# Loading Q and K as float32 four heads at a time, with the cast on GpSimd and all stores on one queue

## The chip, the cores and the metric

The kernel runs on one core of a Trainium2 chip. The metric is the time of one execution on the device in microseconds (us). The profile gives a span (first to last instruction), which is about 1.9 us shorter than the time of the same execution.

## The reference

```python
q, k: float32, shape (8, 12, 1024, 64)          # 96 heads in all
out = np.einsum('bhid,bhjd->bhij', q, k)         # float32, shape (8, 12, 1024, 1024)
```

The inputs are 50.33 MB together and the output is 402.65 MB, 4 MB (4,096 KB) for each head. Writing the output is nearly all of the work.

## The kernel before

For each head, Q and K are loaded by two DMAs of GpSimd's queue that cast float32 to float16 on the way, transposed on TensorE, and multiplied. VectorE and ScalarE (ACT) move the 512-wide results from PSUM (the memory that TensorE writes its results to) into a 4 MB output tile, and one DMA stores it.

```python
in_pool  = ... bufs=24      # float16 Q and K of one head each: 12 heads ahead
out_pool = ... bufs=5       # output tiles of 4 MB
for bh in range(96):
    q_sb = in_pool.tile([P, NT, D], F16); k_sb = ...        # P=128, NT=8, D=64
    nc.gpsimd.dma_start(out=q_sb, in_=qf[bh].rearrange("(p t) d -> p t d", p=P))
    nc.gpsimd.dma_start(out=k_sb, in_=kf[bh].rearrange("(p t) d -> p t d", p=P))
    # ... 4 transposes of Q, 16 of K (each K block twice, for both halves of the array),
    # ... copied to qT_sb and kT_sb by VectorE (cut) ...
    o_sb = out_pool.tile([P, NT, S], F32)
    for n in range(2):
        for t in range(NT):
            # ... matmul to ps [P, 512]; copy to o_sb by VectorE (7) or ACT (9) (cut) ...
    out_eng = nc.sync if bh % 2 == 0 else nc.scalar
    out_eng.dma_start(out=of[bh].rearrange("(p t) j -> p (t j)", p=P), in_=o_sb)
```

A partition of a load is 8 rows of 64 numbers: 2 KB read, 1 KB written. A partition of a store is one contiguous run of 32 KB. So each store is 128 packets of 32 KB, 8 for each of 16 DMA engines (the trace has 12,288 such packets for 96 heads).

## Time and profile before

| | before |
|---|---|
| median of its first 3 runs | 1075.96 us (1073.93 to 1078.4) |
| span of the profiled execution | 1077.5 us |
| busy: TensorE, VectorE, ACT, GpSimd | 61%, 52%, 44%, 9% |
| HBM traffic over the span | 420 GB/s |
| mean store packet (32 KB), fastest class of them | 1224.7 ns, 1213 ns |
| load packets (1 KB written) | 24,576 of about 99 ns |

These are lines of the profile's page of the kernel before. The DMA line has the mean busy share of the 16 DMA engines in tenths, in 40 equal slices of the span, and the GB/s line what they moved, in bytes as they are written (a casting load counts half of what it reads: 25.18 MB in q0's line, of 50.33 MB read). A queue's line has packets, MB, and the time of its packets as a share of 16 engines' span. The last lines are DMA issues: KB each, and the median us from issue to landing.

```profile
span 1077.5 us, 9569 instructions
...
DMA  9999999999999999999999999999999999999998
GB/s 230 391 426 420 428 415 386 422 355 421 422 385 392 422 425 360 421 423 397 367 422 426 347 421 423 386 396 364 421 417 391 393 422 421 353 419 423 353 425 373
...
q1 hardware_dynamic: 6912, 201.33, 43.8%
q10 hardware_dynamic: 6912, 201.33, 43.6%
q0 software_dynamic: 27648, 25.18, 14.5%
q8 instruction: 27, 0.44, 0.1%
...
HBM read 50.33 MB, written 402.65 MB: 420 GB/s over the span
...
out_dram<-o_sb SPq DMA_DIRECT2D x48, 4096.0 KB, 25.6
...
q_sb<-in_q_dram POOLq DMA_DIRECT2D x96, 128.0 KB, 39.5
```

The DMA line says what bounds the kernel: 9 everywhere, 8 in the last slice. Q1 and q10 are the stores of SP and ACT, q0 the loads. The shares add up to more than 100% because several small load packets can be in flight on one engine. A load of 128 KB takes 39.5 us to land: it shares the engines with stores.

From the view of waits of the same kernel (engine, line, what it waited for: us in total, times, longest us):

```profile
ACT o_sb L82 <- PE ps L71: 564.9, 363, 24.3
...
PEld L56 <- DMA k_sb<-in_k_dram: 210.4, 31, 16.9
```

The engines wait for loads, and behind them for each other. As the DMA engines have work nearly all the time, these waits are a result of the bound, not the bound.

The view of windows, with the stretch in us, then each engine's busy time, the granted clock, the DMA share (1.00 is 16 engines) and GB/s:

```profile
core 0: us, PE busy (x) PEld busy (x) DVE busy (x) ACT busy (x) POOL busy (x), PEclk, DMA share, GB/s
...
10.00:20.00 10.00, 8.89 (x43) 2.81 (x41) 7.38 (x13) 6.15 (x12) 7.79 (x15) 1.00 1.28 224
...
1050.00:1060.00 10.00, 0.00 (x0) 0.00 (x0) 0.00 (x0) 0.00 (x0) 0.00 (x0) 0.50 0.99 426
1060.00:1068.00 8.00, 0.00 (x0) 0.00 (x0) 0.00 (x0) 0.00 (x0) 0.00 (x0) 0.50 1.05 451
1068.00:1076.00 8.00, 0.00 (x0) 0.00 (x0) 0.00 (x0) 0.00 (x0) 0.00 (x0) 0.50 0.77 332
```

After compute has ended, the engines drain their last stores at full rate almost to the end. In the packet records, all 16 are busy until 1.6 us before the last store packet ends.

### The profile page before, as it was taken

What the parts mean: (1) busy time and instruction counts of PE and PEld (TensorE: products, weight loads), DVE (VectorE), ACT (ScalarE), POOL (GpSimd) and SP (SyncE); (2) the same over time, 40 slices, a digit from 0 to 9 for tenths busy, and PEclk for the clock granted to TensorE, in tenths of its full rate; (3) what the DMA queues carried; (4) which work ended last, traced back from release to release, by engine and by line L of the source; (5) the groups of instructions that cost most, each with busy time, mean ns of one, the idle gap of its engine ahead of it and who ended that gap; (6) DMA issues with size and microseconds to landing.
All of it is one profiled execution on the core that took longest, in us unless ns stands there. A gap on an engine that the chain in (4) does not pass through costs nothing.

```text
span 1077.5 us, 9569 instructions
## 1 busy us (share of the span) xinstructions
PE 654.1 (61%) x3456; PEld 211.4 (20%) x3456; DVE 564.9 (52%) x864; ACT 469.5 (44%) x865; POOL 102.1 (9%) x198
## 2 busy tenths in 40 slices
PE   6888428458718627817693784665871862684470
PEld 2222102112202202202221221111220220221120
DVE  5686426447618625816473482544761862483360
ACT  4475315336506514615362462434650651463360
POOL 6100001020002002000200200102000100200000
PEclk9995555656556755855555565555655675565555
DMA  9999999999999999999999999999999999999998
GB/s 230 391 426 420 428 415 386 422 355 421 422 385 392 422 425 360 421 423 397 367 422 426 347 421 423 386 396 364 421 417 391 393 422 421 353 419 423 353 425 373
DMA packets 41519, 428.44 MB, mean 398 GB/s; under 512 B 4608, under 2 KB 29184, under 8 KB 29184
## 3 DMA queue, kind: packets, MB, share of 16 engines
q1 hardware_dynamic: 6912, 201.33, 43.8%
q10 hardware_dynamic: 6912, 201.33, 43.6%
q0 software_dynamic: 27648, 25.18, 14.5%
q8 instruction: 27, 0.44, 0.1%
q14 instruction: 20, 0.16, 0.0%
HBM read 50.33 MB, written 402.65 MB: 420 GB/s over the span
## 4 chain that ended last, share of the span: by engine, by line
PE 34%; another core or an unknown queue 25%; DMA 21%; DVE 15%; issue 2%; ACT 1%; POOL 0%; DVEq 0%; POOLq 0%; ACTq 0%
PE ps L71 21%; DMA q_sb<-in_q_dram 13%; DVE o_sb L78 7%; DVE kT_sb L62 6%; PE t_ps L56 5%; DMA k_sb<-in_k_dram 5%; PE t_ps L57 4%; PE t_ps L54 4%; DMA out_dram<-o_sb 3%; DVE qT_sb L61 1%; ACT o_sb L82 1%; POOL q_sb L47 0%; POOL k_sb L48 0%; DVEq L78 0%
## 5 line engine op out<-in xcount | busy, mean ns | idle before, releaser
L82 ACT COPY o_sb<-ps 128x512 f32<-128x512 f32 x864 | 468.2, 595 | 577.4 <-PE ps L71 564.9
L78 DVE COPY o_sb<-ps 128x512 f32<-128x512 f32 x672 | 427.3, 682 | 212.3 <-ACT o_sb L82 124.4
L71 PE MATMUL ps<-kT_sb,qT_sb 64*128 64x512 f16 x1536 | 485.7, 552 | 39.0 <-DVE o_sb L78 29.6
L56 PE MATMUL t_ps<-ident,k_sb 128*64 128x128 f16 x768 | 143.1, 303 | 192.7 <-DMA k_sb<-in_k_dram 192.7
L61 DVE COPY qT_sb<-t_ps 128x512 f16<-128x512 f16 x96 | 40.2, 418 | 269.4 <-PE ps L71 258.6
L54 PE MATMUL t_ps<-ident,q_sb 128*128 128x128 f16 x384 | 68.5, 280 | 160.5 <-DMA q_sb<-in_q_dram 114.2
L57 PE MATMUL t_ps<-ident,k_sb 128*64 128x128 f16 x768 | 151.5, 303 | 0.0
L71 PEld LDWEIGHTS <-qT_sb 64*128 64x128 f16 x1536 | 94.5, 105 | 195.1 <-issue 162.2
L56 PEld LDWEIGHTS <-k_sb 128*64 128x64 f16 x768 | 74.0, 144 | 250.6 <-DMA k_sb<-in_k_dram 210.4
L62 DVE COPY kT_sb<-t_ps 128x1024 f16<-128x1024 f16 x96 | 116.4, 1213 | 0.0
L57 PEld LDWEIGHTS <-k_sb 128*64 128x64 f16 x768 | 76.9, 143 | 107.7 <-issue 107.7
L47 POOL DMA_DIRECT2D q_sb<-in_q_dram x96 | 51.1, 532 | 423.9 <-PE ps L71 146.8
L48 POOL DMA_DIRECT2D k_sb<-in_k_dram x96 | 50.9, 530 | 423.7 <-PE t_ps L57 205.3
L54 PEld LDWEIGHTS <-q_sb 128*128 128x128 f16 x384 | 31.6, 113 | 280.7 <-issue 145.9
L82 ACT ACT_TABLE_LOAD x1 | 1.3, 1283 | 0.7 <-PEq L103 0.7
masks.py:199 POOL TENSOR_SCALAR_AFFINE_SELECT ident<-ident 128x128 f16<-128x128 f16 x1 | 0.3, 305 | 0.1
masks.py:197 POOL MEMSET ident<- 128x128 f16 x1 | 0.2, 204 | 0.3 <-POOLq L103 0.3
L103 POOL MEMSET const-float32-0.0<- 128x1 f32 x1 | 0.1, 98 | 0.2 <-issue 0.2
L103 POOL MEMSET const-bfloat16-1.0<- 128x1 bf16 x1 | 0.1, 101 | 0.0
L103 POOL MEMSET const-uint8-127<- 128x1 uint8 x1 | 0.1, 101 | 0.0
L103 POOL MEMSET const-float32-1.0<- 128x1 f32 x1 | 0.1, 98 | 0.0
## 6 DMA issues: line engine op xcount, KB each, us to landing
out_dram<-o_sb SPq DMA_DIRECT2D x48, 4096.0 KB, 25.6
out_dram<-o_sb ACTq DMA_DIRECT2D x48, 4096.0 KB, 26.8
q_sb<-in_q_dram POOLq DMA_DIRECT2D x96, 128.0 KB, 39.5
k_sb<-in_k_dram POOLq DMA_DIRECT2D x96, 128.0 KB, 34.7
```

What stands on the lines that cost most here:

```text
L47: nc.gpsimd.dma_start(out=q_sb, in_=qf[bh].rearrange("(p t) d -> p t d", p=P))
L48: nc.gpsimd.dma_start(out=k_sb, in_=kf[bh].rearrange("(p t) d -> p t d", p=P))
L54: nc.tensor.transpose(qT_ps[:, e], q_sb[:, 2 * e : 2 * e + 2], ident)
L56: nc.tensor.transpose(kT_ps[0:64, t], k_sb[:, t], ident)
L57: nc.tensor.transpose(kT_ps[64:128, t], k_sb[:, t], ident)
L61: nc.vector.tensor_copy(out=qT_sb, in_=qT_ps)
L62: nc.vector.tensor_copy(out=kT_sb, in_=kT_ps.transpose([0, 2, 1]))
L71: nc.tensor.matmul(ps, qT_sb[h : h + 64, e], kT_j[h : h + 64, n * 512 : (n + 1) * 512],)
L78: nc.vector.tensor_copy(out=o_sb[:, t, n * 512 : (n + 1) * 512], in_=ps)
L82: nc.scalar.copy(out=o_sb[:, t, n * 512 : (n + 1) * 512], in_=ps)
L103: nc = _bacc.Bacc("TRN2", target_bir_lowering=False, num_devices=1)
```

## The change

The intent: fewer and larger load packets (8 KB instead of 1 KB written), loads issued well ahead, wider evictions (1024 instead of 512), and one queue for all stores. A partition holds 32 consecutive rows of a batch of four heads; the rows are put in order by interleaved transposes. The loads move to ACT's queue and stay float32, without a cast on the way, and GpSimd casts each head's slab. The core of the diff, cut:

```diff
-    in_pool = ... bufs=24 ; out_pool = ... bufs=5 ; po_pool = ... bufs=6 ([P, 512])
+    in_pool = ... bufs=3 (four heads) ; half_pool = ... bufs=3 ; out_pool = ... bufs=4 ; po_pool = ... bufs=3 ([P, 1024])
+    sizes = [1, 1, 2] + [4] * 23
-        nc.gpsimd.dma_start(out=q_sb, in_=qf[bh].rearrange("(p t) d -> p t d", p=P))   # float16 tile
-        nc.gpsimd.dma_start(out=k_sb, in_=kf[bh].rearrange("(p t) d -> p t d", p=P))
+            self.q_sb = in_pool.tile([P, GMAX * NT, D], F32, tag="q")
+            self.k_sb = in_pool.tile([P, GMAX * NT, D], F32, tag="k")
+            for src, dst in ((qf, self.q_sb), (kf, self.k_sb)):
+                nc.scalar.dma_start(out=dst[:, : self.R], in_=src[rows].rearrange("(p r) d -> p r d", p=P))
+            nc.gpsimd.tensor_copy(out=q_h, in_=self.q_sb[:, slab])
+            nc.gpsimd.tensor_copy(out=k_h, in_=self.k_sb[:, slab])
+            # transposes of q_h, k_h as before; then copies that interleave:
+            for g in range(G):
+                nc.vector.tensor_copy(out=qT[:, g, :, :, a], in_=t_ps[:, 0:4, ms])
+            nc.vector.tensor_copy(out=kT[:, :, :, a], in_=t_ps[:, 4:12].rearrange("c t (g m) -> c g m t", g=G))
-                ps = po_pool.tile([P, 512], F32)       # 7 copies by VectorE, 9 by ACT
+                ps = po_pool.tile([P, S], F32)         # 3 copies of 1024 by VectorE, 5 by ACT
-        out_eng = nc.sync if bh % 2 == 0 else nc.scalar
-        out_eng.dma_start(out=of[bh]..., in_=o_sb)
+            nc.sync.dma_start(out=of[bh]..., in_=o_sb)
... (batches; loads issued three batches ahead; each batch's transposes run among the scores of the one before) ...
```

## The prediction

> **What bounds it now.** The DMA engines. In the page's 40 slices DMA is at 90% or more in all but the last; PE is busy 61%, DVE 52%, ACT 44%. The trace's packet records show 16 packets in flight practically always; idle DMA time sums to about 7 us: 2.6 us before the first load, 3.2 us near 1013 us (the last loads land late, the stores run dry), 1.4 us at the end. The compute waits (ACT on PE 565 us, weight loads on k_sb 210 us, view of waits) follow from full queues: 1 KB load packets take turns with 32 KB store packets, so loads trickle until stores run low.
>
> **Costs from the trace.** A store packet is 32 KB in 1213 ns undisturbed: 432 GB/s for 16 engines; the Trainium skill (DMA: Bandwidth & Descriptors, "Where 436 GB/s comes from") gives 435 as the ceiling, and the trace agrees. 402.65 MB of stores need 932 us. Loads: 24,576 packets that read 2 KB and write 1 KB, 96 ns each (150 us of 16 engines), but they overlap, up to 20 in flight: effectively 75 to 80 ns. Stores slow a little beside them (mean 1225 ns). The span leaves some 130 us for loads and semaphores, against 116 us for 50.33 MB at 432 GB/s: small packets cost only about 14 us. The halved write traffic of the casting load saved nothing; bytes read set the pace.
>
> **The change.** Load packets become 8 KB (less in the first three batches), a quarter as many; 8 KB packets of the instruction queue took 309 ns, so 6,144 are an estimated 113 to 119 us. The dry stretch near 1013 us should go: an 8 KB load packet per 32 KB store packet gets a fifth of the engines, issued two batches ahead. Against it, a slower start. The first store left after 19.7 us, with prefetching loads filling the time; now about eight heads (4.2 MB, 10 us) are loaded before it, and the first head needs load, cast, transposes, copies and eviction in sequence, about 14 us: 2 to 4 us more idle DMA. A single SP store queue should cost nothing: where one queue was alone the engines stayed full, also across its DMA boundaries.
>
> **Off the path.** Per head (11 us budget): ACT 5 copies of 1024, estimated 1.02 us each from 595 ns for 512: 5.1 us. DVE 3 at 1.2, kT copy 1.2, four 128-column qT copies at 0.28: 6.0 us. PE as before, 6.8 us. GpSimd two 512-element casts; the skill (GPSIMD Engine Reference, 3.1) has 512 elements in 0.77 us at best: 1.6 to 2.2 us. All fit, and four output buffers give 37 us of slack.
>
> **Sum.** Stores 932 to 938, loads 113 to 119, semaphores and instruction fetch 2 to 3, start 5 to 6, end 3: 1055 to 1069. I predict 1060 us (ratio 0.985), 1050 to 1072 in 8 of 10. Chances: over 2% faster 0.16, within 2% 0.78, over 2% slower 0.06.
>
> **What would show it.** DMA at 9 in nearly all slices; HBM about 427 GB/s over the span (420 now); load queue share about 11% (14.5% now); some 6,500 load packets; first store near 14 us; no wait of PE for loads; mean store packet near 1220 ns.
>
> **What would make it wrong.** Faster: large load packets overlap store packets more than small ones. Slower: the chain of cast, transposes, single transpose buffer and DVE copies exceeding 11 us per head at the throttled clock (granted mean 0.60), or bubbles between stores of one queue: then DMA slices below 9 and store waits on DVE or ACT.

## More of the kernel before

The experiments ran on three chips, four kernels to a chip; the kernel before was rerun each time, with medians of 1077.2, 1077.85 and 1077.38 us, so kernels of different groups are compared by their ratios to it.

## The result, and the profile after

| | before | after |
|---|---|---|
| median of 4 runs | 1076.89 us (1073.93 to 1078.4) | 1081.55 us (1080.08 to 1081.68) |
| ratio, 95% interval | 1 | 1.0042 (1.0024 to 1.0060) |
| span of the profiled execution | 1077.5 us | 1079.7 us |

A ratio here and below is the mean time of one kernel's runs over that of the other's of the same rounds, so it is not quite the ratio of the medians. The change is within 2%, as predicted likeliest, but it is slightly slower where 1.5% faster was predicted, and 1081.55 lies outside the range of 1050 to 1072.

The page after:

```profile
span 1079.7 us, 9227 instructions
...
DMA  8999999999999999999999999999999999999993
GB/s 294 428 431 431 425 426 433 426 434 424 430 439 421 431 434 422 434 429 427 434 432 429 433 425 436 427 428 431 429 432 428 426 431 438 429 428 436 429 432 171
...
q1 hardware_dynamic: 13824, 402.66, 86.9%
q10 hardware_dynamic: 7488, 50.33, 11.3%
q8 instruction: 27, 0.44, 0.1%
...
HBM read 50.33 MB, written 402.65 MB: 420 GB/s over the span
...
L79 POOL CAST q_h<-q_sb 128x512 f16<-128x512 f32 x96 | 59.2, 616 | 776.0 <-PE t_ps L83 744.1
...
out_dram<-o_sb SPq DMA_DIRECT2D x96, 4096.0 KB, 36.1
```

In between, the GB/s line is what was hoped for: 421 to 439, without the dips to 347 of before (there the engines ran casting load packets, of which the line counts half the bytes that are read, so a part of the dips is a matter of counting). But the first slice is 8, and the last is 3, with 171 GB/s instead of 373. One slice is 27 us. The waits:

```profile
ACT o_sb L119 <- DMA out_dram<-o_sb: 264.2, 54, 6.9
...
POOL q_h L79 <- DMA q_sb<-in_q_dram: 4.3, 4, 2.3
```

Compute now waits for free output tiles (ACT, 264 us in all), and almost never for loads: GpSimd's casts, their only reader, waited 4.3 us for Q in the whole run, and 2.5 us for K. So stores are always queued ahead, in up to four tiles. The windows:

```profile
10.00:20.00 10.00, 6.91 (x53) 2.89 (x54) 6.27 (x8) 4.49 (x5) 3.84 (x7) 0.97 0.67 256
...
1050.00:1060.00 10.00, 0.00 (x0) 0.00 (x0) 0.00 (x0) 0.00 (x0) 0.00 (x0) 0.50 0.99 426
1060.00:1068.00 8.00, 0.00 (x0) 0.00 (x0) 0.00 (x0) 0.00 (x0) 0.00 (x0) 0.50 0.37 160
1068.00:1076.00 8.00, 0.00 (x0) 0.00 (x0) 0.00 (x0) 0.00 (x0) 0.00 (x0) 0.50 0.07 29
```

From 1068 to 1076 us the DMA share is 0.07, and one engine of 16 is 0.0625: **one DMA engine works alone** on the last stores, at 29 GB/s, and the other 15 have finished. The packet records say the same. In the table, "tail" is the time from the moment at which the first of the 16 engines has no store packet left to the end of the last packet. (On one engine, a packet begins 3 to 4 ns before the end of the one before it. That overlap is taken off, as otherwise 15 engines can count as 16.) The times are on the records' own clock, on which the span begins at about 10.4 us (before) and 10.7 us (after).

| | first store packet | 16 engines busy until | last store packet ends | tail |
|---|---|---|---|---|
| before | 30.1 us | 1085.0 us | 1086.6 us | 1.6 us |
| after | 33.7 us | 1070.1 us | 1088.9 us | 18.7 us |

So the change did work: the engines were kept together for 15 us less (1070.1 against 1085.0), though the first store came 3.6 us later. Then the tail took it all back. (The profiled execution of the kernel before is not among its timed runs, and with 1077.5 us of span it is some 2.5 us slower than their median; so up to 2.5 of the 15 us may be chance.)

The records carry no engine number. But on one engine a packet begins where the one before ended, and a packet of 4 bytes, for the semaphore, follows the 8 packets of each store. So the packets can be chained into 16 sequences. At 866 us, when the loads had ended, one sequence still had 181 store packets to do and the other fifteen had 169 to 174. And the lag grew over the run: the sixteen parts of one store landed within 3.6 us of each other at 45 us, and from 3.1 us early to 10.9 us late, against the median, at 617 us. In the kernel before, the spread was 2.6 us in the median store and never over 5.9 us, and it did not grow.

The chains of the kernel after also say where the lag comes from. From 60 us on, each has 750 or 751 store packets. The late engine's take 1240.8 ns in the mean (up to 1035 us), the others' 1217.6 to 1222.6 ns. Packets of 1230 to 1333 ns cost the late engine about 17 us in all, and the others 0.5 to 2 us each. Instruction fetches are not the reason: this chain has none of 16 KB, and two of 8 KB, one of them after its last store.

### The profile page after: what moved, and what is told of

Same layout as the page of the kernel before. It is cut to its first block, busy times and chain, and to the rows that moved or that the text cites. A ratio compares the mean times of both kernels' runs of the same rounds, so it can differ in the third digit from the quotient of the medians.

```text
span 1079.7 us, 9227 instructions
## 1 busy us (share of the span) xinstructions
PE 672.6 (62%) x3456; PEld 213.2 (20%) x3456; DVE 566.9 (52%) x758; ACT 469.0 (43%) x481; POOL 118.8 (11%) x198
## 3 DMA queue, kind: packets, MB, share of 16 engines
q10 hardware_dynamic: 7488, 50.33, 11.3%
## 4 chain that ended last, share of the span: by engine, by line
DMA 79%; PE 8%; ACT 7%; DVE 2%; issue 1%; ACTq 0%; POOL 0%; SPq 0%
DMA out_dram<-o_sb 75%; PE ps L111 7%; ACT o_sb L119 7%; DMA k_sb<-in_k_dram 3%; PE t_ps L86 1%; DVE kT L97 1%; DVE o_sb L117 1%; DVE qT L96 1%; PE t_ps L83 1%; DMA q_sb<-in_q_dram 0%; PE t_ps L87 0%; ACTq L119 0%; POOL q_h L79 0%; SPq L120 0%
## 5 line engine op out<-in xcount | busy, mean ns | idle before, releaser
L119 ACT COPY o_sb<-ps 128x1024 f32<-128x1024 f32 x480 | 467.7, 1014 | 571.1 <-DMA out_dram<-o_sb 264.2
L111 PE MATMUL ps<-kT,qT 64*128 64x512 f16 x1536 | 524.1, 604 | 235.2 <-ACT o_sb L119 168.0
L117 DVE COPY o_sb<-ps 128x1024 f32<-128x1024 f32 x288 | 352.0, 1223 | 379.8 <-PE ps L111 221.3
L111 PEld LDWEIGHTS <-qT 64*128 64x128 f16 x1536 | 98.5, 109 | 613.6 <-issue 593.8
L96 DVE COPY qT<-t_ps 128x128 f16<-128x128 f16 (+1 forms) x374 | 122.1, 470 | 98.7 <-PE t_ps L87 98.7
L79 POOL CAST q_h<-q_sb 128x512 f16<-128x512 f32 x96 | 59.2, 616 | 776.0 <-PE t_ps L83 744.1
L97 DVE COPY kT<-t_ps 128x1024 f16<-128x1024 f16 x96 | 118.8, 1237 | 0.0
L87 PE MATMUL t_ps<-ident,k_h 128*64 128x128 f16 x768 | 103.9, 312 | 0.0
L86 PE MATMUL t_ps<-ident,k_h 128*64 128x128 f16 x768 | 103.4, 314 | 0.0
L86 PEld LDWEIGHTS <-k_h 128*64 128x64 f16 x768 | 78.7, 167 | 22.0 <-issue 20.8
L87 PEld LDWEIGHTS <-k_h 128*64 128x64 f16 x768 | 78.5, 165 | 5.9 <-issue 5.9
L80 POOL CAST k_h<-k_sb 128x512 f16<-128x512 f32 x96 | 59.1, 616 | 51.5 <-PE t_ps L87 48.6
## 6 DMA issues: line engine op xcount, KB each, us to landing
q_sb<-in_q_dram ACTq DMA_DIRECT2D x23, 1024.0 KB, 17.2
k_sb<-in_k_dram ACTq DMA_DIRECT2D x23, 1024.0 KB, 28.6
```

Source lines behind the costliest of these rows:

```text
L79: nc.gpsimd.tensor_copy(out=q_h, in_=self.q_sb[:, slab])
L80: nc.gpsimd.tensor_copy(out=k_h, in_=self.k_sb[:, slab])
L86: nc.tensor.transpose(t_ps[0:64, 4 + t], rows, ident)
L87: nc.tensor.transpose(t_ps[64:128, 4 + t], rows, ident)
L96: nc.vector.tensor_copy(out=qT[:, g, :, :, a], in_=t_ps[:, 0:4, ms])
L97: nc.vector.tensor_copy(out=kT[:, :, :, a], in_=t_ps[:, 4:12].rearrange("c t (g m) -> c g m t", g=G),)
```

## The experiments

The theories, as they stood before the runs:
- A: one DMA engine is slower than the rest, and the change lets it fall behind. Before, stores ran dry so often that all engines waited for each other; now four tiles are queued and nothing waits.
- B: one SP store queue is the cause.
- C, and F later: the float32 loads themselves are the cause.
- D: the depth of the output buffers lets the lag grow, so fewer would help.
- G: the casts on GpSimd disturb the DMA engines. I: instruction fetches do. R: fetches that fall on one engine do. Q: it is which queue issues the loads.

Every kernel below gave correct results. The edits are against the kernel after.

### e1: stores alternate between SP and ACT again (theory B)

```diff
-            nc.sync.dma_start(
+            (nc.sync if bh % 2 == 0 else nc.scalar).dma_start(
```

> Edit: the changed kernel, but stores alternate between SP and ACT as before. In the trace of the changed kernel 15 of 16 DMA engines finish their last store between 1059 and 1067 us of the span and one runs alone to 1078. Theory A (one engine needs some 2% longer for each store packet while the others run ahead, and nothing in the changed kernel makes them wait for it): no change, 1078 to 1084 us, the tail of about 12 us stays. Theory B (the single SP queue lets the engines drift apart or leaves bubbles): the tail goes, 1064 to 1072 us.

Measured: 1131.7 us, ratio 1.0520 (1.0492 to 1.0547). The DMA and GB/s lines of its page:

```profile
DMA  8989999999999999999989998997998999799998
GB/s 308 399 354 404 431 427 439 423 419 426 426 408 384 424 406 385 407 377 424 400 353 411 426 427 338 426 426 321 410 431 359 410 419 428 319 424 429 427 428 377
```

Both numbers were missed. The tail is gone, as B had it (2.4 us), but B's gain did not come, so B falls. Slices of 7 and 8 appear in the middle: the stores run dry, about every four heads, and at these points a lag is made good (in between, the parts of one store land up to 24 us apart). Two reasons are likely, and no run separates them: two stores now share the engines, so both finish late, and with four tiles there is too little left to fill the gap; and loads sit behind stores in ACT's queue (a 1 MB load of K takes 36.6 us to land here, 28.6 us in the kernel after). The Trainium skill (DMA: Bandwidth & Descriptors, "Rules for kernel authors") says that spreading DMAs over several issuing engines does not help bandwidth; this run agrees, and it cost 5% here, where the loads are on ACT's queue too.

### e2: the loads cast again, four heads at a time, by GpSimd's queue; no casts on GpSimd (theories C, F)

```diff
-            self.q_sb = in_pool.tile([P, GMAX * NT, D], F32, tag="q")     # and k_sb
+            self.q_sb = in_pool.tile([P, GMAX * NT, D], F16, tag="q")     # and k_sb
-                nc.scalar.dma_start(
+                nc.gpsimd.dma_start(
-            nc.gpsimd.tensor_copy(out=q_h, in_=self.q_sb[:, slab])        # and k_h
+            q_h = self.q_sb[:, slab]                                      # and k_h
```

> Edit: the changed kernel with its four-head batches, but loaded by casting GpSimd DMAs straight into float16 tiles, no float32 tiles and no casts on GpSimd. Theory A: load packets still read 8 KB, so the load share stays near 11% and the slow engine still ends last: 1076 to 1084 us with a tail over 8 us. Theory C (the float32 writes of the loads, twice the bytes into SBUF, are what slows store packets): mean store packet falls from 1220 to about 1214 ns, 1065 to 1073 us.

Measured: 1071.04 us, ratio 0.9949 (0.9928 to 0.9971), faster than both kernels. The tail is 10.7 us and the first store packet comes 4.5 us earlier than in the kernel after. A alone had 1076 to 1084 and missed: what the loads do has a part in how far the engine falls behind. C's range holds the time, but not for C's reason: the mean store packet did not fall to 1214 ns, it is 1223.0 ns. This edit changes three things at once (queue, bytes written, GpSimd's work); e5, e6 and e9 take them apart.

### e3: two output buffers instead of four (theory D)

```diff
-    out_pool = ctx.enter_context(tc.tile_pool(name="out_pool", bufs=4))
+    out_pool = ctx.enter_context(tc.tile_pool(name="out_pool", bufs=2))
```

> Edit: the changed kernel with 2 output buffers in place of 4, so no engine can run more than about one store ahead of the slowest. Theory A: the slow engine sets the pace either way; the tail shrinks to under 5 us, the fast engines idle along the way instead, and the time stays within 1% of 1081 (1076 to 1092), more only if the compute of one head (about 8 us) no longer hides behind one store (9.7 us). If the tail were a separate loss (theory D, a one-off delay of one engine that adds to the end), removing it would give 1066 to 1071 us.

Measured: 1109.0 us, ratio 1.0299 (1.0271 to 1.0327). The tail is gone (1.8 us). But the time is paid elsewhere, and more of it: the parts of one store land within 1.7 us of each other in the median, so the engines run in step, and stores run dry. Its GB/s line:

```profile
GB/s 303 428 433 425 386 439 395 407 416 405 435 416 420 418 401 418 402 418 417 401 429 411 415 434 403 419 417 388 437 393 419 416 383 418 417 401 434 420 422 378
```

D, that fewer buffers would be a gain, falls. For A this is a sign, though its number was missed: with few buffers no lag can accumulate, and there is no tail. It is not a measure of the lag, as two tiles also leave compute less room behind the stores, and how the 27 us are shared between the two is not shown.

### e4: one store without the partitions that were taken for the slow engine's (theory A)

```diff
-            nc.sync.dma_start(out=dst, in_=src)
+            parts = [(0, 120), (120, 128)] if bh == 88 else [(0, 128)]
+            for lo, hi in parts:
+                nc.sync.dma_start(out=dst[lo:hi], in_=src[lo:hi])
```

> Edit: the changed kernel, with the store of one head (88) cut into partitions 0 to 119 and 120 to 127. By the Trainium skill (DMA: Bandwidth & Descriptors, section on the semaphore increment) these use the 15 and the 8 lowest engines, so the sixteenth engine is spared 8 packets (9.7 us), the lowest eight get one more each (1.2 us). The skill also says that engines 7 and 15 are usually slower. If the slow engine is number 15: tail falls from 12 us to about 2, time 1070 to 1073 us. If it is another (7 or any other): 1081 to 1084 us. Either way theory A says that the end is set by one engine's queue alone.

Measured: 1100.3 us, ratio 1.0221 (1.0199 to 1.0244), unclear against the 2% line. The time decides nothing. The divided store's packets ran slowly, with about 140 us of engine time lost around it, and two engines ended late instead of one (the tail is 21.9 us). The chains of its trace tell more. After 866 us one chain has 160 store packets, eight fewer than any other (168 to 182): the spared engine. It is not the slow one, whose packets of 1230 to 1333 ns mark it; that one has 182 and ends last. So the slow engine is not the sixteenth, if the parts went to the engines as the page has it.

### e5: the casts on VectorE instead of GpSimd (theory G)

```diff
-            nc.gpsimd.tensor_copy(out=q_h, in_=self.q_sb[:, slab])        # and k_h
+            nc.vector.tensor_copy(out=q_h, in_=self.q_sb[:, slab])        # and k_h
```

> Edit: the changed kernel with its float32 loads, but the two casts of a head run on VectorE instead of GpSimd. The packet records of the changed kernel, strung together by the end of one packet and the start of the next, show that one engine loses some 20 us over the run to store packets of 1230 to 1320 ns while compute is active (others lose about 5), and none once compute has ended. Theory G (GpSimd's work slows that engine): 1068 to 1074 us, tail under 8 us. Theory F (the float32 writes of the loads do): 1078 to 1083. Theory I (the slowing grows with the number of instructions executed, whatever they are): 1079 to 1082. VectorE stays off the path (6.0 us a head, plus two casts at an estimated 0.4 to 0.6 us).

Measured: 1086.07 us, ratio 1.0075 (1.0060 to 1.0091). The tail is 17.7 us, nearly that of the kernel after. G falls. The loss of some 4 us is at the start: the first store packet comes 5.4 us later (39.1 us), as the casts take their turn among VectorE's other work.

### e6: casting loads as in e2, but GpSimd copies float16 to float16 where it cast (theories F, G)

```diff
-            self.q_sb = in_pool.tile([P, GMAX * NT, D], F32, tag="q")     # and k_sb
+            self.q_sb = in_pool.tile([P, GMAX * NT, D], F16, tag="q")     # and k_sb
-                nc.scalar.dma_start(
+                nc.gpsimd.dma_start(
```

> Edit: the changed kernel, but with casting GpSimd DMAs into float16 tiles, and the two GpSimd copies of a head kept (float16 to float16). Against the run without these copies (1071 us) this adds GpSimd work and two instructions a head, but no float32 bytes. Theory G: 1077 to 1082 us, with a tail over 10 us. Theory F: 1070 to 1073. Theory I: 1070 to 1073 (2 of about 96 instructions a head).

Measured: 1071.83 us, ratio 0.9942 (0.9925 to 0.9959), as e2. GpSimd's work costs nothing; the gain of e2 is in the loads. From its windows (same columns as above):

```profile
1050.00:1060.00 10.00, 0.00 (x0) 0.00 (x0) 0.00 (x0) 0.00 (x0) 0.00 (x0) 0.50 0.94 406
1060.00:1068.00 8.00, 0.00 (x0) 0.00 (x0) 0.00 (x0) 0.00 (x0) 0.00 (x0) 0.50 0.15 66
```

There is still a tail, of 9.9 us, about half of that of the kernel after.

### e7: 48 tiny GpSimd instructions more for each head (theory I)

```diff
+            for x in range(24):
+                nc.gpsimd.memset(q_h[:, 0, x : x + 1], 1.0)     # overwritten by the cast after it
+                nc.gpsimd.memset(k_h[:, 0, x : x + 1], 1.0)
             nc.gpsimd.tensor_copy(out=q_h, in_=self.q_sb[:, slab])        # and k_h
```

> Edit: the changed kernel with 48 one-column memsets on GpSimd per head ahead of the casts, into the tiles that the casts then overwrite: about 50% more instructions in the program, few bytes. Theory I: the lag of the slow engine grows by half, 1088 to 1095 us, tail 18 us or more. Theory G: 1080 to 1084. Theory F: 1080 to 1082.

Measured: 1093.03 us, ratio 1.0138 (1.0123 to 1.0153). The number is the one that theory I expected, but the trace shows another way to it, so I is not confirmed. Theory I had it that the many slightly long store packets (16 to 120 ns over 1213 ns) come from fetches; their sum hardly moved, from 35.7 to 39.6 us of engine time. What grew is the sum of the very long ones (over 120 ns), from 49 to 99 us. Each fetch occupies a data engine itself, and GpSimd's fetches fell on one engine: its chain has 32 of 8 KB. But that engine is not the one that ends last. It ends at 1094.6 us; the slow engine ends at 1101.1 us, with one fetch while compute ran. Its slightly long packets cost it 17 us as before, and very long ones about 10 us, where they cost it 0.3 us in the kernel after. So the additional time is a larger lag of the slow engine, but it comes neither from its slightly long packets nor from fetches on it; its very long packets are not explained. The tail is only 19.5 us because the lag stops growing at some 20 us, from 700 us on: by then the other engines wait for output tiles that the slow one still holds.

### e8: both K copies made by GpSimd, so that TensorE needs half as many K transposes (theories I, R)

```diff
-            k_h = half_pool.tile([P, NT, D], F16, tag="kh")               # half_pool: bufs 3 to 2
+            k_h = half_pool.tile([P, NT, 2, D], F16, tag="kh")
-            nc.gpsimd.tensor_copy(out=k_h, in_=self.k_sb[:, slab])
+            for c in range(2):
+                nc.gpsimd.tensor_copy(out=k_h[:, :, c], in_=self.k_sb[:, slab])
-                nc.tensor.transpose(t_ps[0:64, 4 + t], rows, ident)
-                nc.tensor.transpose(t_ps[64:128, 4 + t], rows, ident)
+                nc.tensor.transpose(t_ps[:, 4 + t], k_h[:, t], ident)
```

> Edit: the changed kernel, with k cast twice side by side, so that one transpose of 128 columns gives both halves: 16 fewer TensorE instructions of 72 a head (a sixth of the program, and fewer instruction fetches), one more GpSimd cast a head. Theory I: the lag shrinks by a sixth, 1076 to 1080 us. Theory G: half as much GpSimd work again, 1084 to 1089 us. Theory F: 1079 to 1082 us.

Measured: 1077.85 us, ratio 0.9997 (0.9982 to 1.0012), some 4 us less than the kernel after by the ratios. The instruction queue q8 has fetches of 16 KB, and there are 21 instead of 27. One takes about 930 ns and lengthens the store packet beside it by 400 to 600 ns. The chains of this trace are nearly clean, and show on which engines time goes: four engines without fetches (from 60 us on) ended at 1068.2 to 1071.6 us, eleven with two to seven fetches (of 16 KB, or the other engines' of 8 KB) at 1072.0 to 1080.0 us, and one engine with none of 16 KB and two of 8 KB at 1085.3 us, after about 14 us of slightly long store packets of its own. So engines with fetches end up to 12 us later than those without, but the one that ends last is late for another reason. Its 14 us are a sixth less than the 17 us of the kernel after, which is what theory I expected of a sixth fewer instructions, and what R does not explain. The edit also changes the casts and half_pool, so that the number of instructions is the cause is not shown.

### e9: float32 loads by GpSimd's queue (theories Q, F)

```diff
-                nc.scalar.dma_start(
+                nc.gpsimd.dma_start(
```

> Edit: the changed kernel, float32 tiles and GpSimd casts kept, but the loads are issued by GpSimd's queue instead of ACT's. It differs from the 1071.8 us run with casting loads and copies only in the float32 bytes written into SBUF. Theory F (the float32 bytes make the late start and the tail): 1079 to 1083 us. Theory Q (it is the ACT hardware queue beside the SP stores: first store at 23 us of the span, more slow store packets on one engine): 1070 to 1074 us, first store near 19 us, tail near 9 us.

Measured: 1078.01 us, ratio 1.0007 (0.9988 to 1.0025). This lies between, so both have a part. Against the kernel after, only the queue differs: 0.35% or 3.5 us (the first store packet comes 2.6 us earlier; the tail is 18.6 us, as before, so the gain is at the start). Against e6, only what lands differs, float32 or float16 (and with it whether the DMA or GpSimd casts): 0.65% or 6 to 7 us. Its windows:

```profile
1060.00:1068.00 8.00, 0.00 (x0) 0.00 (x0) 0.00 (x0) 0.00 (x0) 0.00 (x0) 0.50 0.24 102
1068.00:1076.00 8.00, 0.00 (x0) 0.00 (x0) 0.00 (x0) 0.00 (x0) 0.00 (x0) 0.50 0.04 17
```

Now compare the packet records with e6. Half of the 16 engines have done their stores at 1071.1 us here and at 1070.6 us in e6; the last store packet ends at 1084.6 and at 1078.6 us. **The float32 landing costs the engines as a group next to nothing. It costs the last one 6 us, and it is the last one that counts.** The slightly long packets of that engine (1230 to 1333 ns) cost it about 17.5 us here and 11.6 us in e6. After the loads have ended its mean packet is the same in both, 1239.5 and 1239.3 ns, so the difference arises while loads run.

### e10: e6 and e8 together (theory R)

The edit is the two diffs of e6 and e8, without e8's change of half_pool.

> Edit: casting loads, GpSimd copies that lay k down twice, one transpose in place of two. Theory R (instruction fetches, 16 KB for TensorE and 8 KB for the others, land on single engines and delay these, and fewer instructions mean fewer fetches): as the doubling took 3.7 us off the changed kernel, it takes 2 to 5 us off the 1071.8: 1067 to 1070. If the gain came from something that only the ACT loads have: 1071 to 1073.

Measured: 1069.37 us (1069.31 to 1070.11), ratio 0.9929 (0.9908 to 0.9950), inside what R expected. But R took its number from e8, where the slow engine has no fetch of 16 KB, as in the kernel after; so the number does not confirm R. This is the best version, 0.7% faster than the kernel before and 1.1% faster than the kernel after (0.9929 against 1.0042). Its tail is 8.6 us:

```profile
1060.00:1068.00 8.00, 0.00 (x0) 0.00 (x0) 0.00 (x0) 0.00 (x0) 0.00 (x0) 0.50 0.19 82
1068.00:1076.00 8.00, 0.00 (x0) 0.00 (x0) 0.00 (x0) 0.00 (x0) 0.00 (x0) 0.90 0.00 1
```

### e11: e10, one qT copy in place of four, and e12's early store

```diff
+            # e10's edits, e12's edit, and
-            for g in range(G):
-                nc.vector.tensor_copy(out=qT[:, g, :, :, a], in_=t_ps[:, 0:4, ms])
+            nc.vector.tensor_copy(out=qT[:, :, :, :, a], in_=t_ps[:, 0:4].rearrange("c e (g m) -> c g e m", g=G))
```

> Edit: casting loads, k laid down twice, one qT copy per head in place of four, and the first head's store in four parts. If the terms add (start 3 us earlier, fetches 2 to 5 us less): 1062 to 1068 us. If the slow engine's remaining slow packets set a floor: 1068 to 1071.

Measured: 1070.76 us, ratio 0.9939 (0.9921 to 0.9957). The terms do not add up: it is no better than e10, though its store packets lost less time to the slightly long class (14.6 us instead of 20.7). The number lies in the range for a floor set by the slow engine, whose own slightly long packets cost about as much as in e10 (8.7 and 9.2 us).

### e12: the first head's store in four parts, each as soon as its rows are done (the late start)

```diff
-            nc.sync.dma_start(out=dst, in_=src)
+            cut = 2048 if bh == 0 else 8192
+            for lo in range(0, 8192, cut):
+                nc.sync.dma_start(out=dst[:, lo : lo + cut], in_=src[:, lo : lo + cut])
```

> Edit: the changed kernel, the store of the first head alone cut into four parts of 8 KB a partition, each issued when its two row groups are evicted. If the end is set by one engine's queue that is busy from its first store to the end, then the time falls by what the first store starts earlier: 3 to 6 us, 1075 to 1079. If the tail absorbs it (the queue of that engine is limited by something later): 1080 to 1082.

Measured: 1079.94 us, ratio 1.0021 (1.0002 to 1.0040). The first part left about 10 us earlier, and the hole at the start is filled, as its window from 10 to 20 us shows (0.67 in the kernel after):

```profile
10.00:20.00 10.00, 6.00 (x58) 2.64 (x54) 6.95 (x8) 4.90 (x6) 3.79 (x7) 0.89 1.01 398
```

It brought about 2 us, less than the expected 1075 to 1079 us, probably because what is stored early displaces loads that had run in that time. The tail stayed, at 19.1 us. So the late start is a small part of the miss.

| | ratio to before | first store packet | first engine done | half of them done | last ends | tail |
|---|---|---|---|---|---|---|
| before | 1 | 30.1 us | 1085.0 us | 1085.1 us | 1086.6 us | 1.6 us |
| after | 1.0042 | 33.7 us | 1070.1 us | 1074.4 us | 1088.9 us | 18.7 us |
| e9: queue | 1.0007 | 31.1 us | 1066.0 us | 1071.1 us | 1084.6 us | 18.6 us |
| e6: float16 lands | 0.9942 | 32.2 us | 1068.8 us | 1070.6 us | 1078.6 us | 9.9 us |
| e10: fewer TensorE instructions | 0.9929 | 31.6 us | 1067.9 us | 1071.7 us | 1076.6 us | 8.6 us |

Each row after the second adds one edit to the one above it. From the kernel after to e10 the 12.2 us are 3.5 for the queue, 6.2 for what lands, 2.5 for e8's edit (by medians; by ratios 3.8, 7.0 and 1.4, as the rows come from different chips). The queue moves all engines alike, by an earlier start. The other two hardly move the middle of the engines; they move the last one.

## Why the prediction was wrong

What it had right:
- **The bound and the packet costs.** DMA bounds the kernel, before and after. The 12,288 store packets took 1220.4 ns in the mean (about 1220 predicted), together 937 us of 16 engines (932 to 938 predicted). Loads took 11.3% of the engines' time (about 11%), in 6,656 data packets (some 6,500) and 832 semaphore writes. With overlap taken off they are about 117.5 us (113 to 119). The Trainium skill's ceiling (DMA: Bandwidth & Descriptors, "Where 436 GB/s comes from", 435 GB/s) was near the rate of undisturbed stores, 32 KB in 1213 ns on 16 engines or 432 GB/s.
- **The dry stretches go.** GpSimd waited for loads for 7 us in all, and PE, which was to have no wait for loads, has none.
- **The single SP queue costs nothing.** Between 60 us and the tail the engines were idle for 0.3 us in all; alternating was slower (e1).
- **Compute is off the path.** GpSimd's cast took 0.616 us, even less than expected. The Trainium skill (GPSIMD Engine Reference, section 3.1) has 0.77 us for 512 elements as its best case, from which the prediction's 1.6 to 2.2 us for two casts was an estimate; here the measurement decides. VectorE's qT copies took 0.47 us where 0.28 was estimated; the head still fits into its 11 us.

What it had wrong:
- **"End 3" is the step that failed.** It assumed that the engines finish together, as they did before. They do not: one of the 16 falls behind by some 21 ns with each of its store packets (1240.8 ns against 1217.6 to 1222.6), and ends 18.7 us after the first. From there to the end of the span, the idle time comes to about 15.5 us of 16 engines, 12.5 more than predicted. The sum as measured is 937 (stores) + 117.5 (loads) + about 2.5 (semaphores, fetches) + 6.3 (start) + 15.5 (end) = 1078.8, against a span of 1079.7 us. With 3 for the end it would be about 1066, inside the range. The other terms came out at the upper ends of theirs, which makes up the rest of the way to 1060.
- **The first store near 14 us** came at 23.0 us of the span (33.7 less 10.7). The idle time at the start is 6.3 us where 5 to 6 were predicted, so the time is hardly touched: loads filled most of it. E12 shows how little it is worth.
- **HBM at 427 GB/s over the span**: it was 420, as before; this is the same miss seen as a mean.
- **"What would make it wrong"** named compute over its budget and bubbles between the stores. Neither came. What came was a spread between the 16 engines, and I had read the profile's DMA share as if there were one engine of 16-fold speed.

Where the expected gain went, then: it was made (15 us earlier for the engines as a group), and given back at the end by one engine. The kernel before had the same kind of engine, and its trace shows its long packets too. From 1040 to 1060 us, until compute ended, one of the chains lost 218 to 316 ns in each 10 us, and the others 52 to 79. But there the loads held back compute and stores ran dry often, so 15 engines kept waiting for the slow one's head to be done, and nothing accumulated. Taking those waits away turned them into a tail. That the waits of before hid the lag is an inference from the two traces; e3, where few buffers force the engines together and the tail is gone at 27 us more time, and e1, where stores run dry and the tail is 2.4 us, support it, but both are slower for other reasons too.

What stays open:
- Why this one engine is slower. Its store packets take about 1237 to 1241 ns while compute runs, and most of them 1213 ns as soon as compute has ended; the others take 1218 to 1223 ns. Its loss fell by a sixth in e8, which has fewer instructions, and grew in e7, which has more; each of these edits changes other things too. Each timed execution has a span and a clock, so each was recorded while it ran; whether the recording has a part in it was not tested. The Trainium skill (DMA: Bandwidth & Descriptors, "Latency and other measured facts") says that engines 7 and 15 are usually slower, with a best guess that is specific to DMAs issued by GpSimd. The pattern of one slow engine agrees. The guess does not fit: the kernel after issues no DMA from GpSimd and has a tail of 18.7 us, and with the same loads on GpSimd's queue (e9) it is 18.6 us. Which number the engine has, the records do not say; e4 speaks against 15.
- Why a float32 landing adds 6 us on that engine alone. The lag was seen on every chip of the experiments (tails of 21.9 us in e4, of 17.7 and 17.2 us in e5 and e8, and of 18.6 and 19.1 us in e9 and e12), so it is not one chip's defect.

## What to carry to other kernels

When a kernel is bound by DMA, look at how the 16 engines end, not only at their mean: a DMA share near 1/16 in the last windows means one engine works alone, and a mean of 9 in every other slice hides it. Taking waits away from a DMA-bound loop removes what kept the engines in step, so part of the gain can come back as a tail; count on the slowest engine's queue and not on bytes over bandwidth. Here casting in the DMA itself, in four-head batches, and fewer TensorE instructions were worth 1.1% against the version with float32 loads (e10).

## What the Trainium skill lacked or had wrong

- DMA: Bandwidth & Descriptors, "Latency and other measured facts": the slower engines are put down, as a guess, to DMAs issued by GpSimd ("SWDGE-specific"). Here one engine lags without any such DMA: a tail of 18.7 us, against 18.6 us with the same loads from GpSimd (e9). Whether it is one of those two engines is not known. What does matter is what the loads write: 9.9 us with float16 (e6).
- The same page, "Bandwidth": it counts the 16 engines as one pool. It lacks that their lags accumulate when stores are queued four deep (18.7 us of tail in a 1080 us kernel), and that with two tiles the tail is gone (1.8 us) and the kernel is still 2.6% slower (1.0299 against 1.0042).
- Runtime: NRT & Kernel Launch, "Instruction fetch mechanics", has the instruction memory refilled by DMA in blocks of 16 KiB. It lacks what this costs the data: 27 fetches of 16 KB, about 930 ns each on a data engine, some 400 to 600 ns more for the store packet beside it, and several of them on the same engine. Other fetches were of 8 KB, and took 309 ns in the median.
- GPSIMD Engine Reference, section 3.1, has 0.77 us for 512 elements as the best case of a tight loop; the cast of 512 elements here took 0.616 us (192 of them). The same passage has loops that are faster still for each element, but it lacks which of them a cast is.
- The same DMA page, "Rules for kernel authors", has it that spreading DMAs over SP and ACT doesn't help. It could add that it can hurt: 1.0520 against 1.0042 with four output tiles and the loads on ACT's queue (e1).
